# Layer 1's input projection in one stage: eight column pairs by eleven block products, four ordinary blocks among them, gates kept in DRAM

## The chip, the cores and the metric

The kernel runs on one core of one Trainium2 chip. The metric is the device time of one execution in microseconds; the median of three runs of the kernel before is 1782.47 us (1780.71 to 1785.07). TensorE (PE) multiplies matrices into PSUM, VectorE (DVE) and ScalarE (ACT) work elementwise, GpSimd (POOL) and SyncE (SP) here mostly issue DMAs. Work on different engines runs side by side; on one engine instructions run in the order in which they were queued.

## The reference

One inference step of a two-layer encoder on 384 token rows (256 of a prompt, 8 x 16 of running streams). Layer 0 is attention of two kinds and is not touched here. Layer 1 is a gated MLP:

```python
p = rmsnorm(h, norm1_g) @ w_in1            # 384 x 2048 by 2048 x 12288
u, v, z = p[:, :4096], p[:, 4096:8192], p[:, 8192:]
v = layernorm(v, ln_g, ln_b)               # over 4096 columns
mixed = spatial_mix(v, w_sp, b_sp)         # per 128-position chunk and group of 256 columns
h = h + (u * mixed * silu(z)) @ w_out1     # 384 x 4096 by 4096 x 2048
y = rmsnorm(h, final_g)
```

The normalised rows of `v` that belong to the running streams are an output too. All is float32.

## The kernel before

**Products.** Tokens are three row blocks of 128 (`NT`), the contraction of 2048 is 16 k-tiles of 128 (`KT`), columns go in blocks of 512. To keep float32 accuracy each operand is split into a high part and a rest: ACT writes `hi` by a copy, DVE writes `lo = raw - hi`, and a product is three matmuls (hi·hi, hi·lo, lo·hi). An ordinary column block (`dense_nat`, L107; in steps `eight`, L1004) takes, per k-tile, one weight tile of 128 x 512 (`wload`, L72, issued by SP; `wunit`, L77, splits it) and nine matmuls (`products`, L93), so 144 matmuls in all. Four buffers hold each of `whi` and `wlo`, five hold `raw`.

**Block products.** `seven` (L934) treats two column blocks as a pair. Token blocks 0 and 1, the two halves of the contraction and the two columns make a 2 x 2 by 2 x 2 product of blocks, done by seven block products in place of eight, after the Strassen-Winograd scheme; token block 2 is multiplied as usual in four. Eleven block products of 8 k-tiles by three matmuls replace twelve. The sums of token blocks are made once (`token_sums`, L895). The sums of weight blocks are made by DVE for every pair (`add`, L942, whose line stands for all of them, the closing ones too), and then split (`split2`, L920, by `split`, L89). A pair has three phases of four steps u = 0 to 3, and each step treats four k-tiles:
- `singles` (L945): loads two raw tiles of 128 x 2 x 512, splits both, 24 matmuls.
- `chain` (L961): loads four, adds three times, splits three, 24 matmuls.
- `pair` (L982): loads two, adds once, splits two, 18 matmuls.

After each phase a closing step adds the finished PSUM banks into the two results `v0` and `v1`. Raw tiles (`wide`, L892) have five buffers of 512 KB (`sraw`); the split tiles `shi` and `slo` three each. The PSUM banks of block products come from a pool of four (`bank`), those of ordinary blocks from another four (`dbank`).

**Order.** `run` (L1016) lists steps so that the preparation of a step stands ahead of the matmuls of the step before it. A planner then lays out each engine's queue from the dependencies, the order in the source and its own cost model, and may move instructions past one another; a tile gets its buffer when its first instruction is laid out. Once laid out, a queue is fixed: an instruction that waits holds up those behind it on its engine. `tc.issue_after` keeps what it encloses behind a named instruction on the same engine.

**Stages of layer 1.** (1) `v` columns 0 and 1 as ordinary blocks (L1030, L1031). (2) Two rounds of one pair and one ordinary block of `v` (L1032 to L1042): columns 2, 3 with 6, then 4, 5 with 7; three ordinary k-tiles stand ahead of each chain step and one ahead of each step of the last phase. Every `v` block is stored to DRAM (`vd`, L888) with its statistics for the layer norm taken (`bn_stats`, L887). (3) A loop over eight column blocks c (L1134): an ordinary block of `z` (L1136) with `silu` from PSUM (L1139), an ordinary block of `u` (L1145) gated onto it (L1147), while `v` block c+1 is loaded and normalised (`normalise`, L1057); then spatial mixing (L1166 to L1170), the turn of the gated block by a 32 x 32 transposing DVE instruction and 16 DMAs of POOL (`turn`, L128 to L135), and its split into `ghi`, `glo` (L1177, L1178). After c = 2, 4 and 6, the output projection `out1` (L1102) of the eight k-tiles of two earlier blocks. (4) `out1` of block 6, then the last four k-tiles with the final norm (`last`, L1218), from weights split ahead into `wlast` (L1186).

`slots` has 16 buffers of 128 x 1536 float32, for the residual, the split input and gates, and for results on the way. DVE line L943 with 128x1024 operands is an add of weight tiles, with 128x512 a closing add.

## Time and profile before

| | |
|---|---|
| median of three runs | 1782.47 us |
| the profiled execution | 1781.91 us, of which span 1779.8 us |
| granted TensorE clock, mean | 0.998 of full |
| HBM read, written | 291.64 MB, 35.71 MB |
| stage 2 (two pairs, two ordinary blocks) | about 782 to 972 us of the span |
| stage 3 (eight gated blocks, three `out1`) | about 972 to 1690 us |

The profile names instructions by the kernel's lines and the program's tiles, `out<-in`. A busy PE is not a PE at its peak, since matmuls overlap: what one costs is the distance of starts. In the timeline the columns are start, length, engine, line, operation, tiles, shapes and count, and in brackets the idle time ahead of the instruction with what ended it. `SPq` is SP's issue of DMAs. Groups of lines give count, busy time and mean length in ns, then the idle time before them.

### The profile page before, as it was taken

The page shows a single profiled execution, that of the slowest core. Times are in us where ns is not written, and L with a number is a line of the kernel's source. Part 1 is how long each engine was busy: PE and PEld are TensorE (multiplying, and loading weights), DVE is VectorE, ACT ScalarE, POOL GpSimd, SP SyncE. Part 2 cuts the span into 40 slices and gives each one's busy share as a digit, 9 for nine tenths or more (in the row PEclk, how much of TensorE's full clock was granted, in tenths as well). Part 3 has the DMA queues.
Part 4 walks back from the last instruction along what each step waited for, and adds up shares of the span by engine and source line. Part 5 has one row for each costly group of instructions (what it writes and reads, how often), then busy time and mean ns, then how long its engine had stood idle before and what let it go on. Part 6 is the DMA issues. An engine that isn't in the chain of part 4 may idle for free. (4 is left out here: it accounts for less than half of the span.)

```text
span 1779.8 us, 24513 instructions
## 1 busy us (share of the span) xinstructions
PE 1767.2 (99%) x8515; PEld 1464.4 (82%) x8515; DVE 1030.3 (58%) x1674; ACT 740.9 (42%) x1289; POOL 399.0 (22%) x605
## 2 busy tenths in 40 slices
PE   9999999999999999999999999999999999999998
PEld 8978888888888888888887888888888888888887
DVE  6337565457448354677778556555456545454366
ACT  5435354346337244444443433433333333433344
POOL 6525534223311210100112231321021200220020
PEclk9999999999999999999999999999999999999999
DMA  8788989878868977677885655655455643564453
GB/s 228 198 208 202 274 215 229 236 171 217 234 187 213 258 183 165 183 257 229 262 246 185 220 147 158 180 151 154 130 155 156 167 143 125 160 154 135 155 148 119
DMA packets 195244, 335.31 MB, mean 188 GB/s; under 512 B 23768, under 2 KB 62224, under 8 KB 195120
## 3 DMA queue, kind: packets, MB, share of 16 engines
q1 hardware_dynamic: 135888, 242.15, 46.4%
q0 software_dynamic: 28400, 75.47, 17.3%
q10 hardware_dynamic: 30832, 16.13, 3.1%
q8 instruction: 66, 1.08, 0.3%
q14 instruction: 58, 0.48, 0.1%
HBM read 291.64 MB, written 35.71 MB: 184 GB/s over the span
## 5 line engine op out<-in xcount | busy, mean ns | idle before, releaser
L101 PE MATMUL d<-wlo,slot 128*128 128x512 f32 x2157 | 837.8, 389 | 0.0
L102 PE MATMUL d<-whi,slot 128*128 128x512 f32 x2157 | 837.6, 389 | 0.0
L86 DVE TENSOR_TENSOR wlo<-raw,whi 128x512 fp32r<-128x512 f32 x706 | 483.9, 696 | 579.8 <-ACT whi L84 575.9
L84 ACT ACTIVATE whi<-raw 128x512 fp32r<-128x512 f32 x706 | 443.8, 631 | 793.0 <-PE d L102 732.1
L100 PE MATMUL d<-whi,slot 128*128 128x512 f32 x2157 | 761.4, 390 | 1.5 <-ACT whi L84 1.5
L100 PEld LDWEIGHTS d<-whi,slot 128*128 128x128 f32 x2157 | 404.5, 188 | 89.8 <-ACT whi L84 3.1
L101 PEld LDWEIGHTS d<-wlo,slot 128*128 128x128 f32 x2157 | 405.0, 188 | 84.0 <-DVE wlo L86 1.0
L102 PEld LDWEIGHTS d<-whi,slot 128*128 128x128 f32 x2157 | 404.9, 188 | 84.2 <-DVE slot L278 0.3
L135 POOL DMA_DIRECT2D gTt<-trn x128 | 78.1, 617 | 149.2 <-DVE trn L132 110.9
L90 ACT ACTIVATE shi<-sraw 128x1024 fp32r<-128x1024 f32 x56 | 59.4, 1062 | 73.3 <-PE a L932 61.9
L91 DVE TENSOR_TENSOR slo<-sraw,shi 128x1024 fp32r<-128x1024 f32 x56 | 67.7, 1220 | 12.8 <-ACT shi L90 12.7
L464 POOL DMA_DIRECT2D slot<-d x48 | 44.0, 924 | 132.2 <-DMA d<-slot 54.1
L943 DVE TENSOR_TENSOR sraw<-sraw,sraw 128x1024 f32<-128x1024 f32 x32 | 39.1, 1223 | 31.7 <-DMA sraw<-in_w_in_dram 29.8
L1114 POOL DMA_DIRECT2D wr<-in_w_sp_dram x64 | 35.0, 553 | 83.7 <-DVE wT L1118 76.1
L563 POOL DMA_DIRECT2D slot<-wd x32 | 27.1, 855 | 93.9 <-DMA wd<-pr 32.8
L1068 POOL DMA_DIRECT2D out_dram<-v x8 | 4.5, 558 | 183.8 <-DVE v L1067 183.8
L931 PE MATMUL a<-slo,slot 128*128 128x512 f32 x112 | 43.7, 390 | 0.0
L932 PE MATMUL a<-shi,slot 128*128 128x512 f32 x112 | 43.6, 389 | 0.0
L888 POOL DMA_DIRECT2D vd<-slot x8 | 4.4, 551 | 168.6 <-ACT slot L882 162.8
L930 PE MATMUL a<-shi,slot 128*128 128x512 f32 x112 | 41.9, 389 | 0.0
L1107 DVE TENSOR_TENSOR slot<-d,slot 128x512 f32<-128x512 f32 x48 | 31.7, 686 | 11.6 <-PE d L102 11.5
L524 POOL DMA_DIRECT2D kcache<-in_cache_sb_k_dram x32 | 24.9, 786 | 34.0 <-DVE KT L694 34.0
(303 smaller groups left out, 1579.4 us busy)
## 6 DMA issues: line engine op xcount, KB each, us to landing
raw<-in_w_in_dram SPq DMA_DIRECT2D x576, 256.0 KB, 3.3
raw<-in_w_out_dram SPq DMA_DIRECT2D x175, 256.0 KB, 3.5
sraw<-in_w_in_dram SPq DMA_DIRECT2D x64, 512.0 KB, 4.8
slot<-d POOLq DMA_DIRECT2D x48, 192.0 KB, 6.0
d<-slot ACTq DMA_DIRECT2D x24, 256.0 KB, 4.2
vd<-slot POOLq DMA_DIRECT2D x8, 768.0 KB, 7.1
v<-vd POOLq DMA_DIRECT2D x8, 768.0 KB, 6.9
gTt<-trn POOLq DMA_DIRECT2D x128, 48.0 KB, 4.3
```

The costliest lines, as they stand in the source:

```text
L84: highs.append(S.activation(hi, raw, AF.Copy).ins)
L86: splits.append(V.tensor_tensor(out=lo, in0=raw, in1=f32(hi), op=ALU.subtract).ins)
L90: S.activation(hi_out, src, AF.Copy)
L91: V.tensor_tensor(out=lo_out, in0=src, in1=f32(hi_out), op=ALU.subtract)
L100: PE.matmul(o, lhsT=his[k][:, t], rhs=hi[:, 0, :], start=(k == first), stop=False)
L101: PE.matmul(o, lhsT=his[k][:, t], rhs=lo[:, 0, :], start=False, stop=False)
L102: mm = PE.matmul(o, lhsT=los[k][:, t], rhs=hi[:, 0, :], start=False, stop=(k == last))
L135: G.dma_start(dst[32 * j:32 * j + 32, :, 32 * a:32 * a + 32], trn[32 * a:32 * a + 32, :, 32 * j:32 * j + 32])
L464: r = G.dma_start(blk[32 * j:32 * j + 32].rearrange("p h (a d) -> p (h a) d", d=32), d[:, :, 32 * j:32 * j + 32].rearrange("h (a p) d -> p ...
L930: PE.matmul(o, lhsT=xh, rhs=hi[:, j, :], start=(u + j == 0), stop=False)
L931: PE.matmul(o, lhsT=xh, rhs=lo[:, j, :], start=False, stop=False)
L932: PE.matmul(o, lhsT=xl, rhs=hi[:, j, :], start=False, stop=(u == 3 and j == 1))
```

## The change

All of layer 1's input products but `v` columns 0, 1 and `z`, `u` column 7 now stand in stage 2. Eight pairs run there one after the other: three of `v` (columns 2 to 7), then five in which the two columns of a pair are `z` and `u` of one block c = 0 to 4. Four ordinary blocks (`z` and `u` of c = 5 and 6) are spread among the pairs by k-tiles: per pair two ahead of chain steps 0, 1 and 2, one ahead of step 3, one ahead of step 0 of the last phase. Gates `u * silu(z)` are stored to DRAM (`gd`) and loaded again. `z` and `u` of c = 7 remain as two ordinary blocks after the stage. The preparation of the gated blocks (load, normalise, spatial mixing, turn, split) is a generator, `prepare`, whose pieces are issued at hooks, one every two k-tiles: blocks 0 and 1 beside `z`, `u` of c = 7, and two blocks beside each of the three calls of `out1`. `gTt`, `trn` and the like are no longer shared between uses (`lg`, `vh` have buffers of their own, `gate` has two), and the last weights `wlast` are put into the preparation's buffers.

```diff
-        vd = [dram.tile([P, NT, 512], F32, name=nm("vd")) for _ in range(8)]
+        vd, gd = ([dram.tile([P, NT, 512], F32, name=nm(x)) for _ in range(8)] for x in ("vd", "gd"))
...
+            def evict_z(c, o):
+                zs[c] = nat()
+                for tb in range(NT):
+                    S.activation(zs[c][:, tb, :], o[tb], AF.Silu, scale=rstd[:, tb:tb + 1])
+
+            def gated(z, tb, u):
+                V.scalar_tensor_tensor(out=z[:, tb, :], in0=u, scalar=rstd[:, tb:tb + 1], in1=z[:, tb, :], op0=ALU.mult, op1=ALU.mult)
+
+            def evict_u(c, o):
+                z = zs.pop(c)
+                for tb in range(NT):
+                    gated(z, tb, o[tb])
+                G.dma_start(gd[c], z)
...
-            def seven(c):
+            def seven(a0, a1, row_done, stored):
...
+            def zu_pair(c):
+
+                def row_done(j, z, u, tb):
+                    if j:
+                        gated(z, tb, u[:, tb, :])
+                    else:
+                        S.activation(z[:, tb, :], z[:, tb, :], AF.Silu, scale=rstd[:, tb:tb + 1])
+
+                return seven(2 * CW + c * 512, c * 512, row_done, lambda z, u: G.dma_start(gd[c], z))
...
-            for c, c8 in ((2, 6), (4, 7)):
-                (b1, e1), (b2, e2), (b3, e3) = seven(c)
-                one, close = eight(c8)
-                steps = [(b1, u) for u in range(4)] + [(e1, None)]
-                for u in range(4):
-                    steps += [(one, 3 * u + i) for i in range(3)] + [(b2, u)]
-                steps += [(e2, None)]
-                for u in range(4):
-                    steps += [(one, 12 + u), (b3, u)]
-                run(steps + [(e3, None)])
-                close()
...
+            NP = 5
+            ordinary = [st for c in range(NP, 7) for st in eight(evict_z, c, 2 * CW + c * 512) + eight(evict_u, c, c * 512)]
...
+            for make, c in [(v_pair, c) for c in (2, 4, 6)] + [(zu_pair, c) for c in range(NP)]:
...
+                steps += [(part(0), u) for u in range(4)] + [(closing(0), None)]
+                for i, mix in ((1, (2, 2, 2, 1)), (2, (1, 0, 0, 0))):
+                    for u in range(4):
+                        steps += some(mix[u]) + [(part(i), u)]
+                    steps += [(closing(i), None)]
+            run(steps + some(10 ** 6))
...
-        for c in range(8):
-            wTs = [spatial_weights(2 * c + i) for i in range(2)]
-            o = dense_nat(w_in1, 0, 2 * CW + c * 512, hh_, hl_)
...
+        def prepare(c):
+
+            load_v(c)
+            gate = lp.tile([P, NT, 512], F32, tag="gate", name=nm("gate"))
+            G.dma_start(gate, gd[c])
             wTs = [spatial_weights(2 * c + i) for i in range(2)]
...
+            yield from normalise(c)
+            yield
+            vh, vl = split_values(c)
+            yield
...
+        def hooked(c, n=16):
+            it = both(c)
+            return [lambda: next(it, None) and None for _ in range(n)]
+
+        h = hooked(0)
...
+        G.dma_start(gd[7], z7)
+        for k0 in (0, 8, 16):
...
+            out1(k0, 8, hooked(k0 // 4 + 2))
```

More of the change, by code (lines that the diff above doesn't have):

```diff
@@ new lines, in some, with part, f, closing @@
+            def some(n):
+                r = []
+                while ordinary and (n or ordinary[0][1] is None):
+                    r.append(ordinary.pop(0))
+                    n -= r[-1][1] is not None
+                return r
+            steps = []
+            for make, c in [(v_pair, c) for c in (2, 4, 6)] + [(zu_pair, c) for c in range(NP)]:
+                p = []
+                def part(i, make=make, c=c, p=p):
+                    def f(u):
+                        if not p:
+                            p.extend(make(c))
+                        return p[i][0](u) if u is not None else p[i][1]()
+                    return f
+                def closing(i, part=part):
+                    f = part(i)
+                    return lambda: f(None)
+                steps += [(part(0), u) for u in range(4)] + [(closing(0), None)]
[3 more added lines that the diff above has]
+                    steps += [(closing(i), None)]
@@ L1190, in tile_hybrid_step @@
+        for tag, bufs in (("v", 2), ("v", 2), ("vh", 1), ("vl", 1), ("gate", 2), ("trn", 1), ("gTt", 1)):
+            x = lp.tile([P, NT, 512] if tag in ("v", "vl", "gate") else [P, NT * 4, P], F32R, tag=tag, bufs=bufs, name=nm("wlast"))
+            x = x if tag in ("v", "vl", "gate") else x.rearrange("p x q -> p (x q)").rearrange("p (t c) -> p t c", t=NT)
             units += [x[:, j, :] for j in range(NT)]
@@ L1198, in tile_hybrid_step @@
         evicted = out1(24, 4, [lambda: None] * 2 + [last_split] * 3 + [lambda: None] * 3)
[L1200 removed]
+        for _ in range(4):
             x = slot()
             units += [x[:, j * 512:(j + 1) * 512] for j in range(3)]
[L1203 removed]
+        with tc.issue_after(splits[-1]), tc.issue_after(highs[-1]):
             while len(order) > 9:
```

143 lines of the change are left out of this document (71 added, 72 removed).

## The prediction

> **What bounds the kernel now.** First the page's head and its table of engines, then the table of stretches (columns: stretch, length, then busy time and count of PE, PEld, DVE, ACT, POOL, granted clock, DMA share, GB/s).
>
> ```profile
> span 1779.8 us, 24513 instructions
> PE 1767.2 (99%) x8515; PEld 1464.4 (82%) x8515; DVE 1030.3 (58%) x1674; ACT 740.9 (42%) x1289; POOL 399.0 (22%) x605
> ```
> ```profile
> 840.00:880.00 40.00, 40.00 (x178) 33.14 (x177) 32.13 (x41) 18.36 (x23) 1.59 (x3) 1.00 0.74 243
> 920.00:960.00 40.00, 38.32 (x167) 30.85 (x166) 29.86 (x34) 16.81 (x20) 1.87 (x3) 1.00 0.67 215
> ```
>
> PE is the bound: busy 99% of the span, and 178 matmuls in 40 us of the block-product stage (840 to 880). Only 920 to 960 has fewer, 167. What a matmul costs is read from starts, not from its duration of 0.39 us, since matmuls overlap. The timeline of PE:
>
> ```profile
> 810.49 0.39 PE L930 MATMUL a<-shi,sumh 128*128 128x512 f32 x1
> ...
> 814.57 0.39 PE L930 MATMUL a<-shi,slot 128*128 128x512 f32 x1
> ...
> 874.64 0.39 PE L931 MATMUL a<-slo,sumh 128*128 128x512 f32 x1
> ...
> 957.00 0.39 PE L930 MATMUL a<-shi,sumh 128*128 128x512 f32 x1
> 959.04 0.50 PE L931 MATMUL a<-slo,sumh 128*128 128x512 f32 x1 [1.66 <-DVE slo L91]
> ```
>
> Between 810.49 and 814.57 stand 18 starts, so **one matmul is a slot of 0.227 us**. At 959.04 is the only stall in this stage: 2.04 us from start to start, 1.8 us more than a slot, and DVE's split is the releaser. So PE sets the time as long as DVE keeps it fed, and DVE has failed once already.
>
> **What the change takes from PE.** A dense pair of 512-column blocks is 2 x 16 k-tiles x 9 = 288 matmuls. The groups of lines, shapes apart, give the block form:
>
> ```profile
> L931 PE MATMUL a<-slo,slot 128*128 128x512 f32 x112 | 43.7, 390 | 0.0
> L931 PE MATMUL a<-slo,sumh 128*128 128x512 f32 x64 | 25.0, 391 | 1.7 <-DVE slo L91 1.7
> L86 DVE TENSOR_TENSOR wlo<-raw,whi 128x512 fp32r<-128x512 f32 x706 | 483.9, 696 | 579.8 <-ACT whi L84 575.9 <-DMA raw<-in_w_out_dram 2.7
> L90 ACT ACTIVATE shi<-sraw 128x1024 fp32r<-128x1024 f32 x56 | 59.4, 1062 | 73.3 <-PE a L932 61.9 <-issue 4.7 <-DVE sraw L943 2.7
> L91 DVE TENSOR_TENSOR slo<-sraw,shi 128x1024 fp32r<-128x1024 f32 x56 | 67.7, 1220 | 12.8 <-ACT shi L90 12.7
> L943 DVE TENSOR_TENSOR sraw<-sraw,sraw 128x1024 f32<-128x1024 f32 x32 | 39.1, 1223 | 31.7 <-DMA sraw<-in_w_in_dram 29.8
> ```
>
> L931 ran 112 + 64 = 176 times for two pairs, and it is one of three matmuls each time: 264 per pair. A pair saves 24. Pairs go from two to eight, so 6 x 24 = 144 matmuls leave PE, 144 x 0.227 = **32.6 us**. Nothing else on PE changes in number. That is the ceiling of the gain, if nothing else comes to bind.
>
> **What it puts on DVE, ACT and DMA.** Each pair reads every weight twice and adds weight tiles before splitting: by the rows above, per pair, 56/2 = 28 splits (L91) and 32/2 = 16 adds (L943) of 128x1024, and 10 closing adds of 128x512 (by the code). What one costs DVE is read from its starts, in the second pair's chain (the middle phase, four raw tiles a step):
>
> ```profile
> 914.86 1.23 DVE L943 TENSOR_TENSOR sraw<-sraw,sraw 128x1024 f32<-128x1024 f32 x1 [0.27 <-DMA sraw<-in_w_in_dram]
> 916.00 1.22 DVE L91 TENSOR_TENSOR slo<-sraw,shi 128x1024 fp32r<-128x1024 f32 x1
> 917.14 0.69 DVE L86 TENSOR_TENSOR wlo<-raw,whi 128x512 fp32r<-128x512 f32 x1
> 918.17 1.23 DVE L943 TENSOR_TENSOR sraw<-sraw,sraw 128x1024 f32<-128x1024 f32 x1 [0.34 <-DMA sraw<-in_w_in_dram]
> 919.31 1.22 DVE L91 TENSOR_TENSOR slo<-sraw,shi 128x1024 fp32r<-128x1024 f32 x1
> 920.45 0.69 DVE L86 TENSOR_TENSOR wlo<-raw,whi 128x512 fp32r<-128x512 f32 x1
> 921.19 1.23 DVE L943 TENSOR_TENSOR sraw<-sraw,sraw 128x1024 f32<-128x1024 f32 x1
> 922.33 1.22 DVE L91 TENSOR_TENSOR slo<-sraw,shi 128x1024 fp32r<-128x1024 f32 x1
> 925.16 1.23 DVE L943 TENSOR_TENSOR sraw<-sraw,sraw 128x1024 f32<-128x1024 f32 x1 [1.61 <-DMA sraw<-in_w_in_dram]
> ```
>
> A wide operation occupies 1.14 us (914.86 to 916.00), 0.08 less than its duration; a 512-wide one then some 0.60 us (an estimate, 0.69 less 0.09). With the new mix of half an ordinary block (8 k-tiles) per pair, DVE has 44 x 1.14 + 10 x 0.60 + 8 x 0.60 + 2 to 4 us for statistics or gating (three to six more of 128x512) = 63 to 65 us per pair, and PE has (264 + 72) x 0.227 = 76.2 us. In the kernel before, a pair ran with a whole ordinary block: 50.2 + 6.0 + 9.6 + 5.4 = 71 us of DVE beside (264 + 144) x 0.227 = 92.5 us of PE. **DVE's spare time falls from 21 to about 12 us a pair.** ACT has 28 x 1.06 + 8 x 0.63 + some 4 us, about 40 of 76 us: covered.
>
> [...]
>
> DMA carries 32 loads of 512 KB, 8 of 256 KB and a store, 19.7 MB in 76.2 us = 259 GB/s, beside the 243 GB/s at a share of 0.74 in the row for 840 to 880: some 0.8. Bandwidth holds; what it does to the landing time is open.
>
> **Where DVE can fail PE.** Averages hide the order of events. Only three buffers hold split tiles (`shi`, `slo`) and five the raw ones, so DVE can't run far ahead. Take the two phases without spare time.
>
> Chain: the rows above run one step, from the add at 914.86 to that at 925.16, in 10.30 us, with just two ordinary splits: 8.0 us of work and 2.3 us of waits for raw tiles. The new mix gives PE 24 + 18 = 42 slots = 9.52 us for such a step, and 33 slots = 7.48 us for the last. At the old pace the three intervals of a chain lose 2 x 0.78 + 2.2 = 3.8 us; by DVE's work alone (8.0, and 7.4 with one split) they lose nothing.
>
> Pair phase (the last), again DVE:
>
> ```profile
> 869.13 1.23 DVE L91 TENSOR_TENSOR slo<-sraw,shi 128x1024 fp32r<-128x1024 f32 x1 [0.95 <-ACT shi L90]
> ...
> 935.59 3.49 DVE L91 TENSOR_TENSOR slo<-sraw,shi 128x1024 fp32r<-128x1024 f32 x3
> ...
> 942.82 1.23 DVE L943 TENSOR_TENSOR sraw<-sraw,sraw 128x1024 f32<-128x1024 f32 x1 [3.14 <-DMA sraw<-in_w_in_dram]
> ...
> 956.63 1.23 DVE L943 TENSOR_TENSOR sraw<-sraw,sraw 128x1024 f32<-128x1024 f32 x1 [3.62 <-DMA sraw<-in_w_in_dram]
> ...
> 964.14 1.23 DVE L91 TENSOR_TENSOR slo<-sraw,shi 128x1024 fp32r<-128x1024 f32 x1 [0.54 <-ACT shi L90]
> ```
>
> In the second pair the chain's last tile is ready at 935.59 + 3.49 = 939.08 and the pair phase's last at 965.37: 26.3 us, 6.8 of them in the two long waits. It held five ordinary splits; now there is about one: 23.9 us at the old pace. PE now needs 81 slots = 18.4 us between these tiles. Loss 5.5 us at the old pace; by work alone (12 x 1.14 + 4 x 0.60 + 0.60 = 16.7 us) none.
>
> Against a loss stands the lead with which a tile is ready before PE reads it: 870.36 (the split of 869.13) to 874.64, 4.3 us, which the first phase wins back, as it asks DVE for 9 us of 21.8. At the old pace a pair would stall PE 3.8 + 5.5 - 4.3 = **5.0 us; the other end is 0**. Below nothing is excluded: a stall can't make PE quicker. I take 2 us, below the middle, because part of the old pace was PE's own: ACT waited 61.9 us for PE to free split buffers (L90's row), and that slack closes when PE asks for tiles sooner. The rest is a loop through the raw buffers (split done, SP issues, DMA lands, add, split), which doesn't close. Eight pairs: **16 us**, bounds 0 and 40.
>
> **The moved gating stage.** Spatial mixing ran beside eight pairs of dense blocks; now all eight preparations run beside two dense blocks and three calls of the output projection, two in each 65 us (288 slots).
>
> ```profile
> L1107 DVE TENSOR_TENSOR slot<-d,slot 128x512 f32<-128x512 f32 x34 | 22.7, 687 | 10.9 <-PE d L102 10.7
> L132 DVE STREAM_TRANSPOSE trn<-gate 128x1536 f32<-128x1536 f32 x7 | 12.4, 1773 | 0.2
> ```
> ```profile
> 1000.00:1640.00 640.00, 640.00 (x2844) 530.34 (x2843) 343.67 (x544) 234.56 (x393) 107.77 (x184) 1.00 0.52 152
> 1045.48 9.88 POOL L135 DMA_DIRECT2D gTt<-trn  x16 [1.25 <-DVE wlo L86]
> ```
>
> From 1000 to 1640 DVE was busy 343.7 us; less the splits of some 300 k-tiles (2844 matmuls, nine to a k-tile, some of them spatial) at 0.69, L1107 and some 15 us of gating, about 100 us are left for seven preparations (seven turns at L132), some 14 each. Two of them, 32 splits and 12 evictions come to 28 + 22 + 8 = 58 of 65 us: full, not over. POOL issues 16 pieces of each turn in 9.9 us, besides its loads, well inside 32 us. The normalising loads, POOL's queue and DVE's splits are behind one another here, and the second preparation of each group is used early in the next group: three hand-overs, 0 to 10 us each (the upper end is a turn's whole issue time uncovered). I take 1 us each, **3 us**, since PE lost nothing between 1000 and 1640 (640.00 busy, 178 matmuls per 40 us) with the same chain. The round trip of the gates through DRAM and the extra final buffers I cost at nothing: most stores have a stage's time to land.
>
> **Sum.** The profiled execution took 1781.9 us, of which 1779.8 are span; the median of the three runs is 1782.5. Span: 1779.8 - 32.6 - 1.8 (the old stall) + 16 + 3 = 1764.4; with the 2.1 us around it 1766.5, and 0.6 up to the median: **1767 us**. About 0.3% (5.3 us) is what a measurement of this kernel tells from no change.
>
> **Rivals.**
> - *PE stays fed.* Stalls under 1 us a pair, as the averages say (63 to 65 of 76.2 us). 1782.5 - 34.4 plus 0 to 9: 1748 to 1757. Against it: the waits of 3.14 and 3.62 us.
> - *The gain is given back.* DVE keeps the old pace, 3.5 to 5 us a pair; 1782.5 - 34.4 + 28 to 40 = 1776 to 1788, no change.
> - *The raw loop sets the pace, slower than before.* Place: five raw buffers, DVE blocked in its queue behind an add whose tile hasn't landed, with finished halves waiting behind it. It decides once landing takes longer than now, 4.7 us:
>
> ```profile
> sraw<-in_w_in_dram SPq DMA_DIRECT2D x58, 512.0 KB, 4.7
> ```
>
>  With six such waits a pair (four chain steps, two in the pair phase), each extra microsecond costs 6 us a pair on top of 5.0: 1782.5 - 34.4 + 8 x 11 = 1836; half a microsecond gives 1812. For it: a higher DMA share; against it: the share rises only from 0.74 to 0.8.
> - *The clock falls.* If every pair had a pause after which 15 slots ran at half speed, 8 x 3.4 = 27 us come on top of the forecast: 1794. The only such pause on record, 2.04 us, left the clock at 1.00 in the row for 920 to 960. [...]
>
> **How the numbers follow.** Forecast (1757 to 1777) 0.44; fed 0.22; given back 0.16; raw loop 0.14; clock 0.04. Range 1748 to 1790: it holds the first three, 0.82, and both ends of the stalls. Faster by over 0.3% (under 1777) is forecast and fed, 0.66; within 0.3% 0.16; slower 0.18.
>
> **What would show it.** Right: 8371 matmuls of PE in place of 8515, slots still 0.227 us; L931 stalls `<-DVE slo L91` of some 16 us in all, most in the last phase of pairs; L943 waiting for `sraw` of 60 to 120 us in all (29.8 now, for two pairs); landing still near 4.7 us. A count of waits at PE near nothing speaks for the fed case, landing beyond 5.5 us for the raw loop, a granted clock under 1.00 in mid-kernel for the last. Long PE waits for `slot` tiles of the output projection would show the hand-overs mis-sized. I am wrong if the planner orders DVE's splits ahead of its adds (then less), or if PE waits for a closing add to free its bank (then more).

## The result, and the profile after

The changed kernel takes **1833.4 us** (median of 4, 1831.0 to 1839.9) beside 1782.0 us of the kernel before on the same chip: ratio 1.0292, interval 1.0259 to 1.0324. Forecast were 1767 us, with a range of 1748 to 1790: the sign is wrong, and the time is far outside the range.

The head of the page of the changed kernel:

```profile
span 1834.0 us, 24238 instructions
PE 1757.6 (96%) x8371; PEld 1441.5 (79%) x8371; DVE 1238.9 (68%) x1806; ACT 798.4 (44%) x1271; POOL 406.1 (22%) x621
```

The 144 matmuls did go: 8371 in place of 8515. But PE is idle now, and its busy time hides most of it, as a matmul counts 0.39 us while its slot is 0.227. Lost time is therefore read from the table of stretches: length less matmuls x 0.2267 us. Stretches of the changed kernel (stretch, length, then busy time and count of PE, PEld, DVE, ACT, POOL, granted clock, DMA share, GB/s): the whole stage of pairs, the singles and the chain of pair 3 with ordinary matmuls beside them, the chain of pair 5 without, and what follows the last pair:

```profile
781.50:1474.20 692.70, 660.65 (x2843) 531.70 (x2841) 532.11 (x558) 303.83 (x341) 21.30 (x40) 1.00 0.74 239
960.60:988.40 27.80, 27.80 (x124) 23.03 (x123) 16.69 (x18) 11.28 (x14) 1.13 (x2) 1.00 0.76 253
988.40:1029.90 41.50, 40.24 (x172) 31.66 (x171) 36.39 (x39) 18.42 (x21) 0.53 (x1) 1.00 0.77 248
1162.20:1193.30 31.10, 24.33 (x98) 17.18 (x96) 27.32 (x26) 14.25 (x15) 0.00 (x0) 1.00 0.75 238
1474.20:1516.00 41.80, 10.64 (x28) 8.01 (x28) 23.44 (x44) 7.75 (x15) 29.93 (x53) 0.59 0.61 190
```

The stage loses 692.7 - 2843 x 0.2267 = **48.2 us**, 6.0 a pair, where the stage of before lost 2.2. The 42 us behind it hold 28 matmuls, 6.3 us of work: **35.5 us** lost at the hand-over, as the passage from the stage of pairs to the preparation of the gated blocks is called below. Some 6 us more go in the last output products (1600 to 1720), with the 256-column matmuls of spatial mixing counted as half a slot there (0.12 us from start to start, 1629.39 to 1629.51); elsewhere they count as whole slots, which understates a hand-over's loss by 1 to 2 us. 1782 - 32.6 + 46 + 35.5 + 6 = 1837, beside 1835.7 us of the profiled execution: the time is found within 2 us, nearly all of it in two places.

PE's waits in the changed kernel (what waits, for what: sum, times, longest), two groups of lines and the landing time of the raw tiles:

```profile
PE a L946 <- DVE slo L91: 21.5, 23, 3.1
PE d L100 <- ACT slot L1239: 18.0, 1, 18.0
PE a L1209 <- ACT vh L90: 16.7, 3, 13.1
PE a L945 <- DVE slot L958: 5.5, 6, 2.4
```
```profile
L91 DVE TENSOR_TENSOR slo<-sraw,shi 128x1024 fp32r<-128x1024 f32 x224 | 270.6, 1218 | 41.8 <-ACT shi L90 41.1
L958 DVE TENSOR_TENSOR sraw<-sraw,sraw 128x1024 f32<-128x1024 f32 x128 | 156.5, 1222 | 114.5 <-DMA sraw<-in_w_in_dram 105.2
sraw<-in_w_in_dram SPq DMA_DIRECT2D x256, 512.0 KB, 4.6
```

L958 is now the line of `add`, L945 to L947 are the block products, L1239 is the silu of `z` column 7 and L1209 spatial mixing. The raw tiles landed as fast as before (4.6 us, 4.7 then), and DVE's adds waited for them all the same, 105 us in all. PE waited for a closing add to free its bank too, 5.5 us in six waits.

**Inside the stage** the losses lie in the chains. Counted from PE's starts in the timeline, pair by pair, a chain running from its second product to the second product of the last phase, so that the wait for that phase's first split falls to the chain:

| pair | 1 | 2 | 3 | 4 | 5 | 6 | 7 | 8 |
|---|---|---|---|---|---|---|---|---|
| matmuls in the chain (96 are the pair's own) | 167 | 170 | 171 | 151 | 96 | 168 | 172 | 138 |
| lost in the chain, us | 0.0 | 1.6 | 2.7 | 6.4 | 9.3 | 4.1 | 3.3 | 6.5 |
| lost in the last phase, us | 1.6 | 1.3 | 2.0 | 1.7 | 1.2 | 1.1 | 2.0 | 1.7 |

Another 1.9 us went in the first phase of pair 2. The planner pulled ordinary k-tiles ahead of their listed places: early chains got 8 (72 of their matmuls), pair 5 none. DVE in the chain of pair 5:

```profile
1175.71 1.23 DVE L958 TENSOR_TENSOR sraw<-sraw,sraw 128x1024 f32<-128x1024 f32 x1 [1.30 <-DMA sraw<-in_w_in_dram]
1176.85 1.22 DVE L91 TENSOR_TENSOR slo<-sraw,shi 128x1024 fp32r<-128x1024 f32 x1
1177.99 1.22 DVE L958 TENSOR_TENSOR sraw<-sraw,sraw 128x1024 f32<-128x1024 f32 x1
1179.12 1.22 DVE L91 TENSOR_TENSOR slo<-sraw,shi 128x1024 fp32r<-128x1024 f32 x1
1180.72 1.23 DVE L958 TENSOR_TENSOR sraw<-sraw,sraw 128x1024 f32<-128x1024 f32 x1 [0.38 <-DMA sraw<-in_w_in_dram]
```

Adds and splits follow each other 1.14 us apart with short waits between. A chain is 12 adds, 12 splits and 4 half-wide closings: 24 x 1.14 + 4 x 0.60 (one closing occupies 1163.85 to 1164.45) = 29.8 us of DVE, against 96 x 0.2267 = 21.8 us of PE. Without ordinary matmuls beside it (a bare chain, as it is called below) a chain can't keep PE fed, whatever the average of the pair.

**At the hand-over** the timeline of PE, then that of POOL and ACT:

```profile
1473.99 0.39 PE L947 MATMUL a<-shi,suml 128*128 128x512 f32 x1
1487.52 1.89 PE L1209 MATMUL a<-vh,wTh 128*128 128x512 f32 x4 [13.14 <-ACT vh L90]
...
1509.98 0.80 PE L100 MATMUL d<-whi,slot 128*128 128x512 f32 x1 [18.02 <-ACT slot L1239]
1510.58 0.63 PE L101 MATMUL d<-wlo,slot 128*128 128x512 f32 x1
1511.00 0.63 PE L102 MATMUL d<-whi,slot 128*128 128x512 f32 x1
```
```profile
1465.25 0.54 POOL L1117 DMA_DIRECT2D v<-vd  x1 [68.46 <-DVE slo L91]
...
1478.85 0.56 POOL L1123 DMA_DIRECT2D lg<-in_sgu_ln_g_dram  x1
...
1495.51 1.84 POOL L135 DMA_DIRECT2D gTt<-trn  x3
```
```profile
1507.60 1.76 ACT L1221 ACTIVATE slot<-gTt 128x384 fp32r<-128x384 f32 x4 [11.05 <-DMA gTt<-trn]
1509.26 1.82 ACT L1239 ACTIVATE slot<-d,rstd 128x512 f32<-128x512 f32 x3
```

The preparation of the first gated block begins only now: its tiles lie where the stage's tiles lay, so its first load waited 68 us for the last splits (POOL, 1465.25), and its norm weights were asked for at 1478.85. Meanwhile PE has nothing: the `z` block of column 7, which was listed as its cover, has already run inside the stage. The count shows it: eight pairs and 64 k-tiles are 8 x 264 + 64 x 9 = 2688 matmuls, and the stage's row has 2843, 155 more, the 144 of that block and the first of the `u` block of column 7. The silu that frees those banks (L1239) stands on ACT behind the gate's split (L1221), which waits 11 us for the turn.

### The profile page after: what moved, and what is told of

Read it like the earlier page. It is cut to its first block, busy times and chain, and to the rows that moved or that the text cites. A ratio compares the mean times of both kernels' runs of the same rounds, so it can differ in the third digit from the quotient of the medians.

```text
span 1834.0 us, 24238 instructions
## 1 busy us (share of the span) xinstructions
PE 1757.6 (96%) x8371; PEld 1441.5 (79%) x8371; DVE 1238.9 (68%) x1806; ACT 798.4 (44%) x1271; POOL 406.1 (22%) x621
## 5 line engine op out<-in xcount | busy, mean ns | idle before, releaser
L101 PE MATMUL d<-wlo,slot 128*128 128x512 f32 x1581 | 615.5, 390 | 0.6 <-DVE wlo L86 0.6
L102 PE MATMUL d<-whi,slot 128*128 128x512 f32 x1581 | 613.7, 390 | 0.0
L100 PE MATMUL d<-whi,slot 128*128 128x512 f32 x1581 | 573.7, 392 | 18.3 <-ACT slot L1239 18.0
L86 DVE TENSOR_TENSOR wlo<-raw,whi 128x512 fp32r<-128x512 f32 x514 | 351.5, 694 | 309.3 <-ACT whi L84 304.8
L84 ACT ACTIVATE whi<-raw 128x512 fp32r<-128x512 f32 x514 | 321.7, 629 | 485.8 <-PE d L102 417.0
L90 ACT ACTIVATE shi<-sraw 128x1024 fp32r<-128x1024 f32 x224 | 237.5, 1061 | 333.4 <-PE a L947 262.5
L100 PEld LDWEIGHTS d<-whi,slot 128*128 128x128 f32 x1581 | 297.7, 188 | 84.1 <-ACT slot L1239 18.3
L102 PEld LDWEIGHTS d<-whi,slot 128*128 128x128 f32 x1581 | 297.4, 188 | 62.4 <-DVE slot L278 0.3
L91 DVE TENSOR_TENSOR slo<-sraw,shi 128x1024 fp32r<-128x1024 f32 x224 | 270.6, 1218 | 41.8 <-ACT shi L90 41.1
L958 DVE TENSOR_TENSOR sraw<-sraw,sraw 128x1024 f32<-128x1024 f32 x128 | 156.5, 1222 | 114.5 <-DMA sraw<-in_w_in_dram 105.2
L946 PE MATMUL a<-slo,slot 128*128 128x512 f32 x448 | 176.2, 393 | 4.0 <-DVE slo L91 3.9
L947 PE MATMUL a<-shi,slot 128*128 128x512 f32 x448 | 175.4, 392 | 0.0
L945 PE MATMUL a<-shi,slot 128*128 128x512 f32 x448 | 168.6, 392 | 0.0
L945 PE MATMUL a<-shi,sumh 128*128 128x512 f32 x256 | 100.7, 395 | 9.1 <-DVE slot L958 5.5
L947 PE MATMUL a<-shi,suml 128*128 128x512 f32 x256 | 100.1, 391 | 0.0
L945 PEld LDWEIGHTS a<-shi,slot 128*128 128x128 f32 x448 | 84.7, 189 | 17.9
L947 PEld LDWEIGHTS a<-shi,slot 128*128 128x128 f32 x448 | 84.7, 189 | 17.5
```

Of the source, the lines that this page charges most:

```text
L84: highs.append(S.activation(hi, raw, AF.Copy).ins)
L86: splits.append(V.tensor_tensor(out=lo, in0=raw, in1=f32(hi), op=ALU.subtract).ins)
L90: S.activation(hi_out, src, AF.Copy)
L91: V.tensor_tensor(out=lo_out, in0=src, in1=f32(hi_out), op=ALU.subtract)
L100: PE.matmul(o, lhsT=his[k][:, t], rhs=hi[:, 0, :], start=(k == first), stop=False)
L101: PE.matmul(o, lhsT=his[k][:, t], rhs=lo[:, 0, :], start=False, stop=False)
```

## The experiments

Two theories of the stage were set against each other at first. One is VectorE's own work (its adds). The other is the raw loop: a raw tile's buffer is free for the next load only after its add and split, and there are five. A third, the filler theory, laid the loss to ordinary matmuls (the filler beside a chain) that stand in the wrong place. For the hand-over, the theories were a missing cover (no other work for PE during the preparation), or a preparation that is late anyway.

### z of column 7 held back (a_pin)

```diff
-                split(hi, lo, raw)
+                final[:] = [S.activation(hi, raw, AF.Copy), V.tensor_tensor(out=lo, in0=raw, in1=f32(hi), op=ALU.subtract)]
...
-        o = dense_nat(w_in1, 0, 2 * CW + 7 * 512, hh_, hl_, between={kp: h.pop(0) for kp in range(0, KT, 2)})
+        with tc.issue_after(final[0].ins), tc.issue_after(final[1].ins):
+            o = dense_nat(w_in1, 0, 2 * CW + 7 * 512, hh_, hl_, between={kp: h.pop(0) for kp in range(0, KT, 2)})
```

> The changed kernel with one edit: the z block of column 7, which stands behind the stage of pairs, may be placed only behind the last weight split of that stage. Cover theory (some 37 us are lost at the stage's end because the planner spent this block inside the stage, so that nothing lies beside the preparation of the first gate): the waits of 13 us and 18 us for the tiles vh and slot go, the clock stays at 1.00 there, and the time falls by 25 to 37 us to 1796 to 1808; the stage loses at most some 5 us, where those matmuls filled it. Rival (the hand-over is long because the preparation is late and long, by its DMA queue and its buffers, whatever lies beside it): TensorE only waits elsewhere, the time stays at 1826 to 1836.

Measured 1816.2 us, ratio 1.0202 (1.0187 to 1.0217): 17 us less than the changed kernel and short of the 25 to 37 expected. Stretches of the stage and of what follows:

```profile
781.40:1446.80 665.40, 630.52 (x2690) 503.00 (x2689) 520.78 (x541) 295.02 (x327) 21.38 (x40) 0.99 0.75 241
1446.80:1520.00 73.20, 65.23 (x281) 53.54 (x280) 47.35 (x82) 26.18 (x46) 36.22 (x64) 0.93 0.77 232
```

The hand-over's loss fell from 35.5 to 9.5 us (73.2 - 281 x 0.2267), and the stage, without those matmuls as filler, loses 55.6 in place of 48.2. So the missing cover accounts for 26 us, and 7 of them return to the stage. The 13 us wait is gone; one of 8.0 us for L1241 (the silu, behind the gate's split on ACT) is left.

### Other blocks in the two roles (b_vord), and both edits (c_pinvord)

```diff
-            NP = 5
-            ordinary = [st for c in range(NP, 7) for st in eight(evict_z, c, 2 * CW + c * 512) + eight(evict_u, c, c * 512)]
+            NP = 7
+            ordinary = [st for c in range(4, 8) for st in eight(evict_v, c, CW + c * 512)]
...
-            for make, c in [(v_pair, c) for c in (2, 4, 6)] + [(zu_pair, c) for c in range(NP)]:
+            for make, c in [(v_pair, c) for c in (2,)] + [(zu_pair, c) for c in range(NP)]:
```

> The changed kernel with other blocks in the two roles: the four ordinary blocks are v 4 to 7, whose four result tiles leave at once, the pairs are one v pair and seven zu pairs. Same number of matmuls. Filler theory (the stage loses 48 us since the ordinary z blocks hold a result tile until their u block is done and so stop the ordinary blocks, leaving chains with no ordinary matmul beside them): the ordinary matmuls spread otherwise, the loss follows the count of ordinary matmuls beside each chain, and the sum of the stage's losses falls to 15 to 30 us; the time falls by 15 to 30 us to 1803 to 1818 if the hand-over is unchanged. Raw-loop theory and VectorE theory (the loss is set by the pairs' own loads or adds whatever lies between): each pair still loses 6 us, the time stays within 5 us of 1833.

> Both edits: the z block of column 7 held behind the stage, and v 4 to 7 as the ordinary blocks. If the two losses are separate (cover at the stage's end, filler within it), the two gains add up: 1770 to 1790. If one block only moves the loss from one place to the other, it is no better than the better one of the two alone.

Measured 1824.0 us, 1.0254 (1.0226 to 1.0281), and with both edits 1813.8 us, 1.0182 (1.0164 to 1.0199). The stage's loss goes from 48.2 to 39.7 us and, with the pin, from 55.6 to 53.6: small gains, short of the 15 to 30 expected, and the two edits don't add up: c_pinvord is only 2 us under a_pin. The loss still follows the matmuls beside a chain (in b_vord chains with 167 to 181 lose 0 to 2.0 us, those with 106 and 135 lose 7.1 to 7.5), so ordinary `z` blocks that hold a result tile are not the reason why chains run short. What is left as an explanation is too little filler, 64 k-tiles for eight chains; h_np3 and k_np3 below test it.

### Without the additions of weight tiles (d_noadd)

```diff
-                    add(b12, b12, b11, ALU.subtract)
-                    add(b22, b22, b12)
-                    add(b21, b22, b21, ALU.subtract)
+                    for x in (b11, b12, b22, b21):
+                        V.tensor_copy(x[:, 0, 0:1], x[:, 0, 1:2])
...
-                    add(b12, b22, b12)
```

> The changed kernel with the weight tiles' additions left out (32 full-width additions of VectorE by 1-column copies in every pair; the block products are then of plain weights, so the output differs): loads, splits and matmuls are the same. VectorE theory (the adds' 1.14 us each, in the queue ahead of the splits, delay the products): the 34 us lost in the chains and most of the 13 us in the last phases go, the time falls by 35 to 48 us to 1785 to 1798. Raw-loop theory (five raw tiles and a landing of 4.6 us set the pace): the stall stays within 10 us of 48, the time at 1823 to 1836. Filler theory: between the two, as a chain without filler has 96 slots, 22 us, for 16 loads of 512 KB each at the rate of the stage.

The block products then are of plain weights, and the output differs; loads, splits and matmuls stay. Measured 1797.6 us, 1.0097 (1.0077 to 1.0117): 36 us less than the changed kernel. Stretches of the whole stage and of its only bare chain:

```profile
782.00:1437.90 655.90, 648.15 (x2843) 532.36 (x2841) 404.70 (x559) 305.21 (x343) 21.12 (x40) 1.00 0.78 253
1149.90:1176.90 27.00, 23.72 (x97) 17.44 (x96) 17.19 (x27) 13.86 (x15) 0.00 (x0) 1.00 0.78 259
```

The stage loses 11.4 us in place of 48.2; every chain with 156 or more matmuls loses 0 to 1.5. The bare chain still takes 27.0 us for 22 us of matmuls with DVE busy 17; its copies waited 11.7 us for raw tiles, so there the loads set the pace. The run speaks for VectorE's theory, but is no proof against the raw loop, since a raw tile that needs no add is also given back sooner.

### Ordinary k-tiles held at their listed places (f_fill)

The edit stands on top of a_pin.

```diff
+                    with ExitStack() as order:
+                        for i in final:
+                            order.enter_context(tc.issue_after(i.ins))
-                    ws = [wunit(w_in1[k * P:(k + 1) * P, c0:c0 + 512], 1, 512)]
+                        ws = [wunit(w_in1[k * P:(k + 1) * P, c0:c0 + 512], 1, 512)]
```

> The kernel a_pin (1816) with one more edit: the split of each ordinary k-tile may be placed only behind the weight splits of the pair step that is listed ahead of it, so that ordinary matmuls can't be pulled out of the chains in which they are listed. Filler theory (bare chains of 96 matmul slots lose 8 to 10 us because the ordinary k-tiles were used earlier; chains with 160 and more lose 0 to 4): every chain gets some 159 slots and loses 2 to 3 us, the stage loses some 30 us instead of 52 and the time falls by 15 to 25 us to 1791 to 1801. Loop theory (VectorE's total of some 64 us a pair and the raw tiles lose the same wherever the fill stands): the last phases and singles lose what the chains win, the time stays at 1811 to 1820.

Measured 1837.7 us, 1.0312 (1.0293 to 1.0330): 21 us **slower** than a_pin. The filler theory as stated falls. Stretches of the stage and of pair 3's chain:

```profile
782.30:1471.30 689.00, 640.76 (x2690) 517.63 (x2689) 520.45 (x541) 292.81 (x327) 22.41 (x40) 0.97 0.72 234
979.60:1019.50 39.90, 36.10 (x151) 28.90 (x149) 30.12 (x32) 14.82 (x16) 0.00 (x0) 0.96 0.67 221
```

The loss is 79.2 us, 9.9 a pair. Of the eight k-tiles two ran ahead of the chain's first product, as listed, so every chain had 150 matmuls in place of the 159 expected and lost 5.8 to 8.1 us, and the last phases had no filler and lost 1.4 to 4.8. Even spreading came out worse than eight k-tiles here and none there. The edit also fixes where the ordinary splits stand in the queues of ACT and DVE; how much of the 21 us that makes was not tried. And DVE isn't full in such a chain: 30.1 of 39.9 us, while its adds waited 9.7 us for raw tiles:

```profile
L959 DVE TENSOR_TENSOR sraw<-sraw,sraw 128x1024 f32<-128x1024 f32 x10 | 12.2, 1223 | 9.8 <-DMA sraw<-in_w_in_dram 9.7
```

That points to the raw loop after all.

### One addition of each chain step on GpSimd (g_pool)

This edit, too, stands on top of a_pin.

```diff
-                    add(b21, b22, b21, ALU.subtract)
+                    G.tensor_tensor(out=b21, in0=b22, in1=b21, op=ALU.subtract)
```

> The kernel a_pin (1816) with the third addition of each chain step (4 of 16 additions of a pair) on GpSimd, which is idle in this stage, in place of VectorE. A GpSimd add of 128x384 takes 1.06 us in the profile of before, so one of 128x1024 is estimated at 2.8 us. VectorE theory (its 6.8 us of adds and splits in a chain step against 5.4 us of 24 matmuls): 4 x 1.14 = 4.6 us less on VectorE in each chain, the chains' losses of 8 to 9 us fall to 4 to 5 and the small ones go; the time falls by 15 to 30 us. Rival (the latency of load, adds and split decides, as a raw tile is given back only behind its split): the slower add holds the raw tiles 1.7 us longer, nothing is won or some 5 to 10 us are lost: 1811 to 1826.

Measured 1829.4 us (1819.9 to 1833.4), 1.0280 (1.0263 to 1.0297), slower than a_pin; the spread leaves the size open. Groups of DVE and POOL (L938 is the split, L985 the moved add):

```profile
L938 DVE TENSOR_TENSOR slo<-sraw,shi 128x1024 fp32r<-128x1024 f32 x224 | 306.6, 1381 | 49.5 <-ACT shi L938 48.6
L985 POOL TENSOR_TENSOR sraw<-sraw,sraw 128x1024 f32<-128x1024 f32 x32 | 90.6, 2832 | 282.7 <-DMA sraw<-in_w_in_dram 191.9 <-DVE slo L938 38.8 <-DVE wlo L86 24.3
```

While GpSimd adds, DVE's splits get longer: 1.38 us in the mean in place of 1.22, 306.6 - 224 x 1.219 = 33.5 us in all, or 1.05 us for each of the 32 adds moved, against 1.14 saved. The mean hides two kinds: of the stage's 222 splits 21 took 2.2 to 3.4 us, all of them while a GpSimd add ran, and every other one 1.22. Almost nothing is taken off DVE in effect, and the run says nothing against VectorE's theory.

### Six raw tiles (i_raw6, then j_raw6)

Both stand on top of a_pin. In i_raw6 the room came from a smaller pitch of all split tiles (`WPITCH` 528 in place of 576), in j_raw6 from the stage's own alone and from `w16`, allocated later:

```diff
-                return vp.tile([P, 2, 512], F32, tag="sraw", bufs=5, name=nm("sraw"))
+                return vp.tile([P, 2, 512], F32, tag="sraw", bufs=6, name=nm("sraw"))
...
-                hi, lo = (vp.tile([P, 2 * WPITCH], F32R, tag=tag, bufs=3, name=nm(tag))[:, :1024].rearrange("p (j c) -> p j c", j=2) for tag in ("shi", "slo"))
+                hi, lo = (vp.tile([P, 1024], F32R, tag=tag, bufs=3, name=nm(tag)).rearrange("p (j c) -> p j c", j=2) for tag in ("shi", "slo"))
```

> The kernel a_pin (1816) with six raw tiles of 512 KB in place of five (room made by a smaller pitch of the split tiles). Raw-loop theory (loads wait for a tile to be split, and VectorE's adds wait 105 us for loads in all): the next load starts a tile earlier, the waits of the adds fall by a third or more, the time falls by 10 to 25 us to 1791 to 1806. VectorE theory: its queue has no room, the adds' waits only become waits elsewhere; within 5 us, 1811 to 1821.

> The kernel a_pin (1816) with six raw tiles in place of five, and nothing changed ahead of the stage (the room comes from the pitch of the stage's own split tiles and from a small tile allocated later). In i_raw6 the stage of pairs lost some 44 us where a_pin lost 56, but all stages ahead of it were 12 us longer with its other pitch. Raw-loop theory: 10 to 14 us less than a_pin, 1802 to 1806; chains without ordinary matmuls still lose 6 to 9 us, as VectorE's 12 adds, 12 splits and 4 closing adds need some 30 us there against 22 us of matmuls. Rival (the pitch of the split tiles took it, or the 12 us were no accident): 1814 to 1822.

i_raw6 took 1820.9 us, 1.0222 (1.0201 to 1.0243), but its first 794 us had taken 781 in a_pin: 12.7 us more went before the stage began, with the smaller pitch, and that hid the answer. j_raw6 took 1812.0 us, 1.0168 (1.0154 to 1.0182). Stretches of the stage and of what follows in j_raw6:

```profile
781.30:1429.50 648.20, 623.95 (x2690) 500.47 (x2689) 521.05 (x541) 296.46 (x328) 18.98 (x37) 1.00 0.76 248
1429.50:1520.00 90.50, 71.35 (x311) 58.73 (x311) 53.68 (x97) 29.10 (x51) 43.46 (x76) 0.89 0.65 200
```

The stage loses 38.4 us in place of 55.6, but the wait for the silu behind the gate's split grew from 8.0 to 19.1 us and took most of it back. DVE's adds in the stage, in a_pin and in j_raw6, and a bare chain of j_raw6 (pair 5):

```profile
L959 DVE TENSOR_TENSOR sraw<-sraw,sraw 128x1024 f32<-128x1024 f32 x128 | 156.5, 1223 | 102.6 <-DMA sraw<-in_w_in_dram 95.1 <-issue 6.8
L958 DVE TENSOR_TENSOR sraw<-sraw,sraw 128x1024 f32<-128x1024 f32 x128 | 156.7, 1224 | 87.4 <-DMA sraw<-in_w_in_dram 75.7 <-issue 11.2
1156.90:1186.00 29.10, 24.43 (x98) 17.14 (x97) 27.58 (x27) 15.08 (x15) 0.00 (x0) 1.00 0.81 265
```

The adds' waits for raw tiles fell from 95.1 to 75.7 us at the same length of an add, and the pitch of the stage's split tiles, the other edit, left the splits at 1.22 us. So one more raw tile is worth 17 us in the stage, as the raw-loop theory had it. Chains with 96 to 105 matmuls still lose 6.5 to 7.3: there DVE is nearly full, 27.6 of 29.1 us.

### Six pairs with full filler (h_np3), then with both losses taken away (k_np3)

h_np3 stands on top of a_pin:

```diff
-            NP = 5
+            NP = 3
...
-                for i, mix in ((1, (2, 2, 2, 1)), (2, (1, 0, 0, 0))):
+                for i, mix in ((1, (3, 3, 3, 3)), (2, (1, 1, 1, 1))):
```

k_np3 has the six raw tiles of j_raw6 besides, and in `prepare`, ahead of the gate's split, two more hooks for block 0, so that the split is listed behind the silu of `z` 7:

```diff
+            if c == 0:
+                yield
+                yield
             hi, lo = slot().rearrange("p (k t) -> p k t", k=4), slot().rearrange("p (k t) -> p k t", k=4)
```

> The kernel a_pin with six pairs in place of eight (three of v, three of z and u) and 16 ordinary k-tiles a pair in place of 8, three in each step of the chain and one in each step of the last phase, as in the kernel before. Four pairs more than before remain, 96 matmuls or 21.8 us. Filler theory: a chain with 200 slots (45 us) covers VectorE's 30 us and the loads, a last phase with 108 slots loses nothing, so the stage loses 0 to 10 us, and with the cover at its end the hand-over 10 us as in a_pin: 1780 - 22 + 5 to 20 = 1763 to 1778, faster than both kernels. Rival (a pair costs 6 us whatever stands beside it): 36 us lost in the stage, 1794 to 1804.

> The kernel h_np3 (1781; six pairs, 16 ordinary k-tiles beside each; it lost 15 us in the stage and 5 us at the hand-over, where the eviction of z 7 stands on ScalarE behind the first gate's split) with six raw tiles, and with that split behind the eviction. If both losses are what they seem: 5 to 8 us less in the stage and 5 us at the hand-over, 1768 to 1772, 0.6% under the kernel before. If the stage's loss in h_np3 is VectorE's alone, only the hand-over's 5 us come: 1775 to 1778.

h_np3 took 1781.4 us, 0.9996 (0.9986 to 1.0006): its stage lost 15 us, its hand-over some 7, and 96 matmuls less (21.8 us) paid just that. k_np3 took **1770.0 us**, 0.9933 (0.9919 to 0.9946), faster than both kernels. Its stage:

```profile
784.70:1344.30 559.60, 556.54 (x2451) 459.31 (x2450) 425.94 (x461) 253.04 (x296) 16.00 (x30) 1.00 0.74 240
```

559.6 - 2451 x 0.2267 = 4.0 us lost in six pairs, and no wait for the silu is left. The rest of the stage's loss and the hand-over's wait were what they seemed.

### Seven pairs (l_np4, q_np4)

Both are k_np3 with `NP = 4`; the mix is (3, 3, 2, 2) and (1, 1, 1, 0) in l_np4, (3, 3, 3, 3) and (1, 0, 0, 0) in q_np4.

> As k_np3, but seven pairs (three of v, four of z and u) with 13 ordinary k-tiles a pair: 24 matmuls or 5.4 us less. Filler theory: with 10 k-tiles in the chain VectorE's 30 us + 6 us of splits + 5 us of closings stand against 42 us of matmuls, about even, so the seventh pair costs what it saves: 1766 to 1774. If a pair's loss grows steadily as the filler shrinks (2.5 us at 16 k-tiles, 7 us at 8), 4 us a pair are lost, 1774 to 1780.

> The kernel l_np4 (1778; seven pairs, 13 ordinary k-tiles a pair, 10 in the chain and 3 in the last phase) with 12 in the chain and 1 in the last phase. If what stands beside the chain decides: chains of some 185 slots lose 0 to 2 us in place of 2 to 5, the time falls by 8 to 12 us to 1766 to 1770, level with k_np3. If the pair's sum decides: within 3 us of l_np4, 1775 to 1781.

1778.3 us, 0.9978 (0.9969 to 0.9988), and 1776.5 us, 0.9965 (0.9954 to 0.9976). Their stages lose 18.7 and 13.5 us: a seventh pair saves 5.4 us and cost more than it saved in both. The question put to q_np4 isn't settled: the planner moved k-tiles again, and from pair 3 to pair 6 its chains had 164 to 170 matmuls, not 185; chains that did have 187 or more lost 0 to 1.3, those with 164 lost 3.3 to 4.2.

### The move alone (m_moved)

Two pairs of `v` as before (columns 4, 5 and 6, 7), everything else ordinary, in the changed kernel's stage and with its gates in DRAM.

```diff
-            NP = 5
-            ordinary = [st for c in range(NP, 7) for st in eight(evict_z, c, 2 * CW + c * 512) + eight(evict_u, c, c * 512)]
+            NP = 0
+            ordinary = [st for c in (2, 3) for st in eight(evict_v, c, CW + c * 512)] + [st for c in range(NP, 7) for st in eight(evict_z, c, 2 * CW + c * 512) + eight(evict_u, c, c * 512)]
...
-            for make, c in [(v_pair, c) for c in (2, 4, 6)] + [(zu_pair, c) for c in range(NP)]:
+            for make, c in [(v_pair, c) for c in (4, 6)] + [(zu_pair, c) for c in range(NP)]:
...
-                for i, mix in ((1, (2, 2, 2, 1)), (2, (1, 0, 0, 0))):
+                for i, mix in ((1, (3, 3, 3, 3)), (2, (1, 1, 1, 1))):
```

> The move alone: the changed kernel's one stage and its gates through DRAM, but two pairs of v only, as in the kernel before, with 16 ordinary k-tiles beside each, and every other block ordinary: the matmul count of the kernel before. Theory that the lost cover at the hand-over is a consequence of the pairs (chains short of filler made the planner fetch the z block of column 7 from behind the stage): the hand-over keeps its cover, 1780 to 1792. Rival (the move itself takes the cover away): 1810 to 1825.

Measured 1795.7 us, 1.0073 (1.0059 to 1.0087), between the two. The matmuls number 8515 again and the two pairs lose 2.1 us as before. PE's waits behind them:

```profile
PE d L100 <- ACT slot L1239: 6.9, 1, 6.9
PE a L1209 <- ACT vh L90: 3.5, 2, 1.8
```

So the move costs 13 us by itself, about half of it in that one queue on ACT. The other 26 us of the hand-over come with the pairs: here, where the chains have full filler, the `z` block stayed in its place, and PE has no wait of 13 us.

### All eight pairs, hand-over mended (o_all8), and without the additions (p_noadd8)

o_all8 is j_raw6 with the two hooks of k_np3; p_noadd8 is a_pin with those hooks and with the additions left out as in d_noadd.

> The kernel j_raw6 (1812; eight pairs, z 7 held behind the stage, six raw tiles) with the first gate's split behind the eviction of z 7. If the wait of 19 us that TensorE has there in j_raw6 is only that queue: 1788 to 1795, of which some 39 us are the stage's loss in short chains, so still slower than before by 0.5%. If the preparation itself is late (its gate load and its transposes through DRAM), TensorE waits elsewhere: 1803 to 1812.

> The kernel a_pin (five raw tiles, eight pairs) with the first gate's split behind the eviction of z 7, and without the additions of weight tiles (1-column copies in their place). If hand-over and additions are all that the changed kernel lost beside the loads' 12 us (d_noadd): 1780 - 32.6 + 12 to 22 = 1759 to 1769, as the forecast's 144 matmuls less would have it. If something else is lost, over 1775.

o_all8 took 1798.0 us, 1.0090 (1.0073 to 1.0107); 14 of the 19 us came. Stretches of its stage and of what follows, then the stage of p_noadd8:

```profile
782.70:1432.10 649.40, 624.02 (x2690) 502.03 (x2689) 521.03 (x541) 296.26 (x328) 18.98 (x37) 1.00 0.76 248
1432.10:1520.00 87.90, 84.47 (x372) 69.15 (x371) 64.63 (x115) 35.30 (x63) 50.09 (x88) 0.98 0.84 251
```
```profile
782.30:1410.20 627.90, 617.61 (x2690) 505.47 (x2689) 392.80 (x542) 295.85 (x327) 21.12 (x40) 0.99 0.78 255
```

The hand-over loses 3.6 us, the stage 39.6: with everything else mended, eight pairs with half an ordinary block each are still slower than before. p_noadd8 took 1770.8 us, 0.9942 (0.9922 to 0.9962), just over the expected 1769; its stage still loses 18.1 us without the additions. Hand-over, additions and the raw loop account for the change; six raw tiles without the additions were not tried.

## Why the prediction was wrong, step by step

**Right.** The slot of 0.227 us (0.231 in i_raw6 ahead of the stage), 144 matmuls less and the ceiling of 32.6 us hold: lost time counted in slots adds up to the spans. Landing stayed at 4.6 us, and the adds' waits for `sraw`, 105 us, lie in the forecast band of 60 to 120. A wide operation occupies DVE for 1.14 us; for a bare chain that makes 29.8 us, and it took 31.1 with five raw tiles (pair 5) and 29.1 with six, some of its adds done ahead.

**The step that failed most in size: the moved gating stage, 3 us.** It took the listed blocks for cover and costed hand-overs at 1 us each. Measured were 35.5 us at the first hand-over and some 6 later. Two things stood in its place: the planner is free to fetch the covering block into a stage that starves (26 us, a_pin), and the eviction that frees PE's banks was queued on ACT behind a split that waits for the turn's 16 DMAs (7 to 19 us: m_moved, j_raw6). The turn goes from one on-chip tile, `trn`, to another, `gTt`, not through DRAM, as o_all8's expectation has it. The prediction said that the normalising loads, POOL's queue and DVE's splits stand behind one another, and gave each hand-over at most 10 us, from a turn's issue time. The first one holds the whole chain of a preparation, which can't even start before the stage's buffers are free.

**The other: the stall in the stage, 2 us a pair.** Measured were 6.0 in the changed kernel and 9.9 in f_fill, the kernel that ran the listed mix. The old pace (3.8 in a chain and 5.5 in a last phase, 9.3 together) came near that sum, though not its parts, 6.7 and 3.3 in f_fill. The fault was what was taken off it: a lead of 4.3 us that would pay, and then part of the pace as PE's own, since ACT waited for PE to free split buffers. Neither shows in f_fill. What the prediction named as the part that doesn't close, the loop through the raw buffers, stayed whole: DVE's waits for raw tiles in a chain of f_fill, 9.7 us for four steps, are the 2.3 us a step of before. And every chain was taken to have its listed filler, where the changed kernel's had 96 to 172 matmuls; most of the loss lay in the chains, not in the last phases. The average of DVE's spare time (12 us a pair) was true and useless: much of it lies in the singles, where DVE was busy 16.7 of 27.8 us in pair 3, and three split tiles can't carry it into the chain.

**The rivals.** "The raw loop sets the pace" (1812 to 1836) named the time that came and half of the place: DVE blocked behind an add whose tile hasn't landed (j_raw6: one tile more, 17 us less). Its condition, a landing over 4.7 us, wasn't needed; the loop cost as much at the old landing, as soon as PE no longer had ordinary matmuls to run meanwhile. "The clock falls" took part as well: 0.59 in the hand-over, where the starts from 1510.58 on are 0.43 us apart. Of its 3.4 us a pair one stretch shows as much, 8 us of a_pin at 0.57 (1122 to 1130); the two in the changed kernel's stage lost about 1.7 us each. The last sign of being wrong came as well, PE waiting for a closing add to free its bank, but for 5.5 us only. Missing among the rivals was the planner moving the cover away.

## What to carry to other kernels

Compare the demands of two engines phase by phase, over a time no longer than the buffers between them can bridge; spare time elsewhere in the loop counts for nothing. Work listed as cover for a later stage is only cover if something holds it there: ask what a planner will do with it when an earlier stage starves. And count lost time in slots, length less instructions times the distance of starts: by busy time the stage's PE was idle for 32 us (692.70 - 660.65), by slots for 48.

## What the runs showed of the hardware

**VectorE's splits got longer beside a GpSimd add.** In g_pool an add of 128x1024 float32 on GpSimd (2.83 us in the mean) lengthened VectorE's splits by about as much as an add costs there, 1.05 us beside 1.14: three splits from 1171.11 on took 5.67 us in place of 3.49 in one chain, with a GpSimd add of 2.59 us from 1171.98 on. What makes them longer no run here shows.

**The clock fell after short waits too, but not after each.** PE's timeline in a_pin, chain of the last pair:

```profile
1414.45 0.50 PE L946 MATMUL a<-shi,sumh 128*128 128x512 f32 x1 [1.83 <-ACT shi L938]
...
1415.71 0.62 PE L948 MATMUL a<-shi,suml 128*128 128x512 f32 x1
1416.13 0.63 PE L947 MATMUL a<-slo,slot 128*128 128x512 f32 x1
```

A wait of 1.83 us, some 7 us behind a few of 0.4 to 0.6, was followed, 1.3 us after its end, by 3.4 us in which starts are 0.43 us apart in place of 0.227 (granted clock 0.79 from 1414 to 1422). The length of the wait alone doesn't decide: in the changed kernel a wait of 1.76 us before 1624.5 was followed by 8 us at 0.79, another of 1.76 us before 1697.8 by full clock (1.00 from 1697.8 to 1705.8), and in f_fill one of 2.51 us before 861.11 by full clock too (1.00 from 861 to 869). What else decides was not shown.

```profile
1624.00:1632.00 8.00, 7.52 (x28) 6.04 (x29) 3.77 (x8) 2.85 (x7) 0.53 (x1) 0.79 0.78 215
```

In the changed kernel the price inside the stage is small: two stretches of 8 us at 0.79 (after 1121 and 1456, behind waits of 2.36 and 3.10 us), about 1.7 us of lost time each.

**With another pitch of the split tiles matmuls were slower.** In i_raw6 everything ahead of the stage took 794 us with split tiles 528 elements apart, 781 with 576. A stretch of 80 us of it, in a_pin and in i_raw6:

```profile
700.00:780.00 80.00, 79.84 (x353) 65.68 (x352) 54.11 (x81) 38.51 (x64) 5.38 (x7) 1.00 0.65 190
700.00:780.00 80.00, 79.93 (x346) 64.56 (x345) 49.15 (x76) 34.72 (x60) 7.06 (x9) 1.00 0.66 177
```

PE waited for nothing in either, at full clock, but its matmuls started 231 ns apart in place of 227. Over the some 2,870 matmuls of L100 to L102 into `d` ahead of the stage (957 of each line in the changed kernel) 4 to 5 ns each are about 13 us. Whether the pitch itself does it, or the addresses that shift with it, was not tried.
